# A two-layer encoder trunk: memory queries turned at tick 4, scores four ticks later, and ScalarE's weight splits queued behind data splits

## The chip, the cores and the metric

The kernel runs on one core of a Trainium2 chip. The metric is the device time of one execution in microseconds (us), the median of several runs. Five engines work side by side, each through its own instruction order: TensorE (PE; its weight loads are listed as PEld), VectorE (DVE), ScalarE (ACT), GpSimd (POOL) and SyncE (SP), which here issues the DMA transfers.

## The reference

The input is x, 256 tokens of width 2048, and 256 memory tokens. Two layers run one after the other, all in float32, and each sub-layer is wrapped in RMS norms before and after:

```python
for layer in range(2):
    hn = rms_norm(h, mix_pre_g[layer])
    if layer == 0:   # 8 neighbourhood heads and 8 sliding-window heads, one input projection
        y = concat(neighbourhood_attention(...), sliding_window_gqa(...)) @ even_w_out
    else:            # 8 heads of differential attention
        y = differential_attention(...) @ odd_w_out
    h = h + rms_norm(y, mix_post_g[layer])
    c = memory_cross_attention(rms_norm(h, mem_pre_g[layer]), rms_norm(mem, ...), wq, wk, wv, wo)
    h = h + rms_norm(c, mem_post_g[layer])
    f = squared_relu(rms_norm(h, mlp_pre_g[layer]) @ w_up) @ w_down      # d_ff = 8192
    h = h + rms_norm(f, mlp_post_g[layer])
```

The memory attention has four heads of 128: q from h, k and v from the memory tokens, a softmax over 256 memory tokens, and an output projection of 512 to 2048.

## The kernel before

**Arithmetic.** Every float32 operand of a matrix product is split in a high and a low part, and each product is three matmuls (`mm3`, L254: high times high, high times low, low times high). Data are split by `split_to` (L397): ScalarE writes the high part (L398), VectorE the low part (L399). Weights are split in `Weights.load` (L177): a DMA brings a tile of 256 x 512 into one of three raw buffers, ScalarE writes the high part and VectorE the low part into one of nine weight buffers `w` (L188 and L189 without a gain; L193 and L194, in two halves, with the gain of the norm multiplied in). A raw buffer is free again when both have read it.

**Blocks.** The tokens are two tiles of 128 (t = 0 and 1). `in_block` multiplies the transposed, normalized stream by one 512-column block of an input projection: eight weight tiles, for each token tile two steps of three matmuls per weight tile. With a lag, tile 1 runs that many weight tiles behind tile 0. `out_block` multiplies attention output or MLP output by 512 rows of an output projection: eight weight tiles, four chunks of 512 columns for each token tile; with `stagger` all chunks of tile 0 come first, and the chunk's result goes to `Leave`, which forms the norm and the new stream.

**Order.** TensorE's order is the order of the program, fixed by hand. A clock of ticks, one tick for a step of three matmuls, decides where small work comes between: `line.later(n, f)` runs f at n ticks from now, `line.when(n, ready, f)` tries at tick n and again each tick until ready, and `line.until(...)` runs what is due at once, with no matmuls between. The order on ScalarE, VectorE and SyncE is not written by hand: a planner takes, when the program is built, what it reckons to be ready, the earlier in the program first. It fixes one order per engine, and the engine then waits at each instruction for what that needs. So a weight split can be placed ahead of data splits that stand before it in the program.

**Weights ahead.** When TensorE's program uses weight tile j, `Weights.get` loads, in program order, up to tile j + 4 (`AHEAD`); at most nine are held.

**The memory block** (`mem_and_mlp`, L654, once per layer). First the query block, `in_block(U["mq", l], ...)` with a lag of 6. As a token tile is finished, `evac_T` (L417) has ScalarE write it, scaled, from PSUM to `q` (L427), and puts its turning `D_EVM` + t = 11 + t ticks later: four transposes on TensorE (L435) and a `split_to` into qT. Then `Heads(...).start(M_AT)`: the scores of head i at tick 8 + 5 i, if qT and kT are there (L257, at<-kT,qT), the softmax, and 9 ticks later the turning of the probabilities (`p_T`, L505) and its split into pT. The value block `mv` with a lag of 5 runs meanwhile, for 32 ticks; then for each head, once its pT has been issued, the mix of probabilities and values (L257, at<-pT,v) and its split into `lt`, then `out_block` of `mo`, staggered, and the MLP. The MLP has 16 groups: `up` makes 512 columns, `split_u` squares and splits them, and `out_block` of `dn` adds the group's output.

Of the kernel before, what the change touches and what calls it, by code (L numbers as in the profile page):

```python
# [3 lines left out]

# [1 line left out]

# [5 lines left out]
F32 = mybir.dt.float32  # L12
F32R = mybir.dt.float32r
BF16 = mybir.dt.bfloat16
AF = mybir.ActivationFunctionType
ALU = mybir.AluOpType
# [5 lines left out]
KT = D // P  # L22
# [12 lines left out]
SW_GAP, SW_T, SW_M = 4, 8, 7  # L35
NA_GAP, NA_T, NA_M = 5, 14, 9
ME_GAP, ME_T, ME_M = 5, 9, 12
D_TRS, D_RMS, D_EVM, D_EVU, M_TR, M_GO = 4, 13, 11, 6, 11, 1
A_ROPE, A_NA, M_AT = 10, 1, 8
A_DF, DF_GAP, DF_T, DF_M, DF_O = 6, 5, 7, 4, 8  # L40
AHEAD = 4
L_MQ, L_MV, L_UP, L_Q = 6, 5, 8, 6
# [29 lines left out]
def trunk(  # L72
# [6 lines left out]
    V, A, G, PE = nc.vector, nc.scalar, nc.gpsimd, nc.tensor  # L79
# [18 lines left out]
    gains = keep.tile([P, P], F32, name="gains")  # L98
# [4 lines left out]
    def mm_ps():  # L103
        return ps.tile([P, 512], F32, tag="mm", bufs=3, name="mm")

    def tr_ps():
        return ps.tile([P, 512], F32, tag="tr", bufs=2, name="tr")
# [15 lines left out]
    class Line:  # L123
        def __init__(self):
            self.now, self.q, self.n = 0, [], 0
# [29 lines left out]
    class Weights:  # L155
        def __init__(self):
            self.specs, self.tiles, self.n, self.wait, self.open = [], {}, 0, [], set()
            self.goal, self.live = -1, 0

        def plan_in(self, src, n0, g, spare=(), gate=None):  # L160

# [15 lines left out]
        def load(self, j):  # L177
            src, k0, n0, tag, _, g = self.specs[j]
            raw = rawp.tile([P, 2, 512], F32, tag="raw", name="raw")
            nc.sync.dma_start(  # L180
                raw, src[k0 * P : (k0 + 2) * P, n0 : n0 + 512].rearrange("(k p) n -> p k n", p=P)
            )
            if tag is None:
                w = wp.tile([P, 2, 2, 512], F32R, tag="w", name="w")
            else:
                w = sb.tile([P, 2, 2, 512], F32R, tag=tag, bufs=1, name="w")
            if g is None:
                A.copy(w[:, 0], raw)  # L188
                V.tensor_tensor(w[:, 1], raw, w[:, 0].bitcast(F32), ALU.subtract)  # L189
            else:  # L190
                for kk in range(2):
                    gk = gains[:, g * KT + k0 + kk : g * KT + k0 + kk + 1]
                    A.activation(w[:, 0, kk], raw[:, kk], AF.Copy, scale=gk)  # L193
                    V.scalar_tensor_tensor(  # L194
                        w[:, 1, kk], raw[:, kk], gk, w[:, 0, kk].bitcast(F32), ALU.mult, ALU.subtract
                    )
            self.tiles[j] = w

        def pump(self):
# [35 lines left out]
    W = Weights()  # L235
# [26 lines left out]
    def in_step(pt, u, kp, t):  # L262
        w = W.get(u + kp)
        line.until(lambda: I.has_x(t, kp // 2, W.specs[u + kp][5] >= G_MN))
        for kk in range(2):
            kt = 2 * kp + kk
            mm3(pt, xT_lhs(kt, t), lambda b: w[:, b, kk, :], kt == 0, kt == KT - 1)
            if kk == 1 and t == NT - 1:
                W.done(u + kp)
            line.tick()  # L270

    def in_block(u, evac, lag=0, between=None):

        pts = {}
        for i in range(8 + lag):
            for t, kp in enumerate((i, i - lag)):
                if not 0 <= kp < 8:
                    continue
                if kp == 0:
                    pts[t] = mm_ps()  # L280
                in_step(pts[t], u, kp, t)
                if kp == 7 and lag:
                    evac(t, pts[t])
                    if between is not None:
                        between(t)
        if not lag:
            for t in range(NT):
                evac(t, pts[t])
# [106 lines left out]


    def split_to(hi, lo, src):  # L397
        A.copy(hi, src)  # L398
        V.tensor_tensor(lo, src, hi.bitcast(F32), ALU.subtract)  # L399

    def scaled_split(dst, t, w, src, r):
# [5 lines left out]
    def rope(tile_, t, nh):  # L407
        v = tile_.rearrange("p (h d) -> p h d", d=DH)
        cos = cst[:, C_COS + t * 32 : C_COS + t * 32 + 32].unsqueeze(1).broadcast_to([P, nh, 32])
        sin = cst[:, C_SIN + t * 32 : C_SIN + t * 32 + 32].unsqueeze(1).broadcast_to([P, nh, 32])  # L410
        u = sb.tile([P, 4, 32], F32, tag="rope", bufs=1, name="rope")
        V.tensor_tensor(u[:, :nh, 0:16], v[:, :nh, 16:32], sin[:, :, 0:16], ALU.mult)
        V.tensor_tensor(u[:, :nh, 16:32], v[:, :nh, 0:16], sin[:, :, 16:32], ALU.mult)
        V.tensor_tensor(v[:, :nh, 0:32], v[:, :nh, 0:32], cos, ALU.mult)
        V.tensor_tensor(v[:, :nh, 0:32], v[:, :nh, 0:32], u[:, :nh], ALU.add)

    def evac_T(dst, r, q=False, roped=0, width=512, ev=None):  # L417


        def f(t, pt):  # L420
            rt = r[t]
            assert rt is not None
            if q:
                rt = sm.tile([P, 1], F32, tag="rs", name="rs", bufs=4)
                V.tensor_scalar_mul(rt, r[t], SCALE)
            u = sb.tile([P, 512], F32, tag="q", bufs=2, name="q")
            A.activation(u[:, :width], pt[:, :width], AF.Copy, scale=rt)  # L427
            if roped:
                rope(u[:, :width], t, roped)

            def turn():
                tp = tr_ps()
                n = width // P
                for i in range(n):
                    PE.transpose(tp[:, i * P : (i + 1) * P], u[:, i * P : (i + 1) * P], ident)  # L435
                d = [dst[:, a, t, 0:n, :].rearrange("p k c -> p (k c)") for a in range(2)]
                split_to(d[0], d[1], tp[:, :width])
                I.wrote(dst, t)

            line.later(D_ROPE + t if roped else (D_EV if ev is None else ev) + t, turn)  # L440

        return f
# [9 lines left out]
    def qT_tile():  # L452
        return sb.tile([P, 2, NT, 4, P], F32R, tag="qT", bufs=1, name="qT")

    def kT_tile():
        return sb.tile([P, 2, NT, 4, P], F32R, tag="kT", bufs=1, name="kT")

    def v_tile():
        return sb.tile([P, 2, NT, 512], F32R, tag="v", bufs=1, name="v")
# [39 lines left out]
    def p_T(p, tag="pT"):  # L499

        pT = sb.tile([P, 2, NT, S], F32R, tag=tag, bufs=2 if tag == "pT" else 1, name="pT")
        tp = at_ps()
        for t in range(NT):
            for kt in range(NT):
                PE.transpose(tp[:, kt * S + t * P : kt * S + (t + 1) * P], p[:, t, kt * P : (kt + 1) * P], ident)  # L505
        d = [pT[:, a].rearrange("p k q -> p (k q)") for a in range(2)]
        split_to(d[0], d[1], tp)
        return pT

    class Heads:  # L510
# [20 lines left out]
        def mix(self, i):  # L531
            v, vh = self.a[3], self.a[4]
            if self.lt is None:
                self.lt = lt_tile()
            o = at_ps()
            for kt in range(NT):
                mm3(
                    o[:, :S], lambda a: v[:, a, kt, vh(i) * DH : (vh(i) + 1) * DH],
                    lambda b: self.pT[i][:, b, kt, :], kt == 0, kt == NT - 1,
                )  # L540
            split_to(self.lt[:, 0, i, :], self.lt[:, 1, i, :], o[:, :S])
            self.n += 1
# [19 lines left out]
    U = {"kv": W.plan_in(w_in, 4096, G_MIX)}  # L562
# [91 lines left out]
    def mem_and_mlp(l, R, kT, nxt):  # L654
        qT = qT_tile()
# [2 lines left out]
            for n in range(4):  # L658
                mem_x(t, n)

        in_block(U["mq", l], evac_T(qT, R, q=True, ev=D_EVM), lag=L_MQ, between=between)
        v = v_tile()
        hd = Heads(qT, kT, lambda i: i, v, lambda i: i, tags=("pT", "pT", "qT", "kT"), lag=(ME_GAP, ME_T, ME_M)).start(M_AT, mix=False)
        in_block(U["mv", l], evac_V(v, RSM), lag=L_MV)
# [7 lines left out]
        R = lv.next  # L672
# [62 lines left out]
        for g in range(NG):  # L735
# [5 lines left out]
            if last:  # L741
                eps = []
                for r in R:
                    q = sm.tile([P, 1], F32, tag="r2", name="r2")
# [9 lines left out]
    R = [None] * NT  # L754
# [52 lines left out]
    qT = qT_tile()  # L807
# [13 lines left out]
    qT = qT_tile()  # L821
# [3 lines left out]
    qT = qT_tile()  # L825
# [9 lines left out]
    qT = qT_tile()  # L835
# [9 lines left out]
    W.free(("mq", 0))  # L845
    out_block(U["oa1"], hd.lt, False, lv, stagger=True)
    R = mem_and_mlp(0, lv.next, kT, G_MIX + 1)


# [85 lines left out]
    qT, kT, v = qT_tile(), kT_tile(), v_tile()  # L935
# [3 lines left out]
    for b in range(4):  # L939
        in_block(U["v", b], evac_V(v, R))  # L940
        hd = DiffHeads(qT, kT, v).start(A_DF)
        if b < 3:
            qT = qT_tile()
# [5 lines left out]
        else:  # L949
# [3 lines left out]
            W.free(("mq", 1))  # L953
            out_block(U["o3"], hd.lt, False, lv, stagger=True)
    mem_and_mlp(1, lv.next, kT, None)


# [27 lines left out]
```

## Time and profile before

| | |
|---|---|
| time, median of 3 runs | 2374.73 us (2373.03 to 2378.61) |
| the profiled execution's own time | 2374.78 us |
| its span (first to last instruction) | 2372.7 us |
| TensorE busy | 2346.2 us (99%), 11687 matmuls |
| VectorE busy | 1611.9 us (68%) |
| ScalarE busy | 1377.7 us (58%) |
| DMA | 451.88 MB, mean 190 GB/s |
| chain that ended last | PE 91%, DMA 3%, DVE 3%, ACT 2% |

A busy share is an average over stages. TensorE's matmuls are pipelined, so the distance from one start to the next tells how fast they are issued, and the duration shown is longer than that. In a timeline, the first two numbers are the start in us from the span's start and the length of the merged piece, and in brackets stands the idle time before it with what ended it.

### The profile page before, as it was taken

How to read it: one execution, taken by the hardware profiler on the slowest of the kernel's cores; microseconds unless marked ns; L12 is line 12 of the kernel's file. 1: busy time of each engine (PE TensorE's matmuls, PEld its weight loads, DVE VectorE, ACT ScalarE, POOL GpSimd, SP SyncE). 2: the span in 40 equal slices, each digit the busy share in tenths (PEclk: the TensorE clock that was granted, in tenths of full speed). 3: DMA queues.
4: the chain of work that ended last, by engine and by line, in shares of the span. 5: the costliest groups of instructions: out<-in, count | busy, mean ns of one | idle time of the engine just before them, and what ended most of it. 6: DMA issues, size and time to landing. Idle time of an engine off the chain costs nothing.

```text
span 2372.7 us, 32033 instructions
## 1 busy us (share of the span) xinstructions
PE 2346.2 (99%) x11687; PEld 1984.9 (84%) x11687; DVE 1611.9 (68%) x2545; ACT 1377.7 (58%) x2280; POOL 28.0 (1%) x46
## 2 busy tenths in 40 slices
PE   8999999999999999999999999999999999999998
PEld 7788887888888888888888888887888888888887
DVE  6776678856666656666876667788666666666666
ACT  6756567765545545545665655577655545555553
POOL 0000000000000000000000000000000000000000
PEclk9999999999999999999999999999999999999999
DMA  7657655565655666665565555655666665665663
GB/s 250 212 183 233 188 193 190 178 209 181 198 193 183 195 196 183 195 197 187 180 195 172 171 188 169 204 178 181 202 195 194 187 195 187 188 199 182 196 195 114
DMA packets 238279, 451.88 MB, mean 190 GB/s; under 512 B 21289, under 2 KB 22185, under 8 KB 237353
## 3 DMA queue, kind: packets, MB, share of 16 engines
q1 hardware_dynamic: 237832, 449.32, 59.7%
q8 instruction: 91, 1.49, 0.3%
q14 instruction: 68, 0.55, 0.1%
q10 hardware_dynamic: 288, 0.52, 0.1%
HBM read 445.59 MB, written 5.15 MB: 190 GB/s over the span
## 4 chain that ended last, share of the span: by engine, by line
PE 91%; DMA 3%; DVE 3%; ACT 2%; issue 1%; POOL 0%; SPq 0%; DVEq 0%; POOLq 0%; ACTq 0%
PE mm L257 59%; PE at L721 14%; PE at L725 7%; PE mm L721 5%; PE mm L725 2%; PE at L257 2%; DVE w L194 1%; DMA raw<-in_even_w_in 1%; PE tr L435 1%; DMA raw<-in_odd_w_in 1%; PE tr L348 1%; ACT w L193 1%; PE at L505 0%; DMA h<-in_x 0%; ACT junk L321 0%
## 5 line engine op out<-in xcount | busy, mean ns | idle before, releaser
L257 PE MATMUL mm<-w,lt 128*128 128x512 f32 x4032 | 926.9, 390 | 0.0
L257 PEld LDWEIGHTS mm<-w,lt 128*128 128x128 f32 x4032 | 754.8, 188 | 155.9
L194 DVE SCALAR_TENSOR_TENSOR w<-raw,gains,w 128x512 fp32r<-128x512 f32 x944 | 678.2, 747 | 261.5 <-ACT w L193 258.7
L193 ACT ACTIVATE w<-raw,gains 128x512 fp32r<-128x512 f32 x944 | 636.0, 717 | 354.1 <-PE mm L257 268.9
L257 PE MATMUL mm<-w,xT 128*128 128x512 f32 x2784 | 674.0, 395 | 2.0 <-DVE v L403 1.1
L189 DVE TENSOR_TENSOR w<-raw,w 128x1024 fp32r<-128x1024 f32 x336 | 411.2, 1224 | 377.6 <-ACT w L188 376.8
L188 ACT CAST w<-raw 128x1024 fp32r<-128x1024 f32 x336 | 353.1, 1051 | 439.1 <-PE mm L725 193.3
L257 PEld LDWEIGHTS mm<-w,xT 128*128 128x128 f32 x2784 | 513.2, 189 | 104.4 <-DVE v L403 1.9
L721 PE MATMUL at<-xT,w 128*128 128x512 f32 x1440 | 368.8, 391 | 0.0
L721 PEld LDWEIGHTS at<-xT,w 128*128 128x128 f32 x1440 | 262.7, 188 | 49.0
L725 PE MATMUL at<-xT,w 128*128 128x256 f32 x1440 | 211.0, 283 | 0.0
L725 PEld LDWEIGHTS at<-xT,w 128*128 128x128 f32 x1440 | 197.2, 191 | 9.4
L312 DVE TENSOR_TENSOR y<-mm,y 128x512 f32<-128x512 f32 x256 | 175.5, 685 | 15.6 <-PE mm L257 15.4
L721 PE MATMUL mm<-xT,w 128*128 128x512 f32 x480 | 147.8, 389 | 0.0
L721 PEld LDWEIGHTS mm<-xT,w 128*128 128x128 f32 x480 | 90.1, 188 | 19.3
L725 PE MATMUL mm<-xT,w 128*128 128x256 f32 x480 | 96.7, 283 | 0.0
L725 PEld LDWEIGHTS mm<-xT,w 128*128 128x128 f32 x480 | 74.9, 192 | 0.0
L679 ACT COPY ue<-at 128x256 f32<-128x256 f32 x90 | 33.7, 374 | 28.0 <-DVE s L680 13.9
L399 DVE TENSOR_TENSOR lt<-s,lt 128x512 fp32r<-128x512 f32 x64 | 44.1, 689 | 3.6 <-ACT lt L398 3.6
L257 PEld LDWEIGHTS at<-kT,qT 128*128 128x128 f32 x240 | 34.5, 191 | 10.5 <-ACT qT L398 4.2
L257 PE MATMUL at<-kT,qT 128*128 128x256 f32 x240 | 37.3, 288 | 5.8 <-ACT qT L398 3.4
L321 ACT ACTIVATE junk<-y 128x512 bf16<-128x512 f32 x32 | 20.1, 629 | 38.5 <-DVE y L307 38.3
(113 smaller groups left out, 1063.6 us busy)
## 6 DMA issues: line engine op xcount, KB each, us to landing
raw<-in_mlp_w_up SPq DMA_DIRECT2D x256, 512.0 KB, 4.1
raw<-in_mlp_w_down SPq DMA_DIRECT2D x256, 512.0 KB, 4.2
raw<-in_odd_w_in SPq DMA_DIRECT2D x96, 512.0 KB, 4.2
raw<-in_even_w_in SPq DMA_DIRECT2D x72, 512.0 KB, 4.3
raw<-in_even_w_out SPq DMA_DIRECT2D x32, 512.0 KB, 4.2
raw<-in_odd_w_out SPq DMA_DIRECT2D x32, 512.0 KB, 3.8
mt<-memT SPq DMA_DIRECT2D x32, 256.0 KB, 4.0
raw<-in_mem_wk SPq DMA_DIRECT2D x16, 512.0 KB, 4.4
```

Source lines behind the costliest of these rows:

```text
L188: A.copy(w[:, 0], raw)
L189: V.tensor_tensor(w[:, 1], raw, w[:, 0].bitcast(F32), ALU.subtract)
L193: A.activation(w[:, 0, kk], raw[:, kk], AF.Copy, scale=gk)
L194: V.scalar_tensor_tensor(w[:, 1, kk], raw[:, kk], gk, w[:, 0, kk].bitcast(F32), ALU.mult, ALU.subtract)
L257: PE.matmul(pt, lhs(a), rhs(b), start=first and i == 0, stop=last and i == 2)
L312: V.tensor_tensor(ysl, pt, ysl, ALU.add)
L348: PE.transpose(pt[:, i * P : (i + 1) * P], h[:, t, k * P : (k + 1) * P], ident)
L399: V.tensor_tensor(lo, src, hi.bitcast(F32), ALU.subtract)
L435: PE.transpose(tp[:, i * P : (i + 1) * P], u[:, i * P : (i + 1) * P], ident)
L679: A.copy(e, pt[:, S:])
L721: PE.matmul(pts[nt], wn, both, start=kp + kk == 0, stop=kp == 7 and kk == 1)
L725: PE.matmul(pts[nt][:, :S], wn, both[:, :S], start=False, stop=False)
```

## The change

Three things are changed. The memory queries' turning has its own delay, `D_EVQ` = 4 ticks (+ t) in place of 11. The memory heads' scores start at tick `M_AT` = 9 in place of 8. And `split_to` remembers its ScalarE instruction in `W.behind`; the splits of a weight tile loaded later in the program are put behind it with `tc.issue_after`. That gives each of the tile's ScalarE instructions an edge in issue order: the planner must place it after that instruction in ScalarE's order. It is no wait of its own, and VectorE's and SyncE's instructions get no edge. Every `split_to` counts: the turnings of q and k, the probabilities, the mixes and the MLP's `split_u`; `split_x` and `scaled_split` don't use it.

```diff
-D_TRS, D_RMS, D_EVM, D_EVU, M_TR, M_GO = 4, 13, 11, 6, 11, 1
-A_ROPE, A_NA, M_AT = 10, 1, 8
+D_TRS, D_RMS, D_EVM, D_EVQ, D_EVU, M_TR, M_GO = 4, 13, 11, 4, 6, 11, 1
+A_ROPE, A_NA, M_AT = 10, 1, 9
...
-            self.goal, self.live = -1, 0
+            self.goal, self.live, self.behind = -1, 0, None
...
-            if g is None:
-                A.copy(w[:, 0], raw)
-                V.tensor_tensor(w[:, 1], raw, w[:, 0].bitcast(F32), ALU.subtract)
-            else:
-                for kk in range(2):
...
+            with tc.issue_after(self.behind) if self.behind is not None else nullcontext():
+                if g is None:
+                    A.copy(w[:, 0], raw)
+                    V.tensor_tensor(w[:, 1], raw, w[:, 0].bitcast(F32), ALU.subtract)
+                else:
+                    for kk in range(2):
...
     def split_to(hi, lo, src):
-        A.copy(hi, src)
+        W.behind = A.copy(hi, src).ins
         V.tensor_tensor(lo, src, hi.bitcast(F32), ALU.subtract)
...
-        in_block(U["mq", l], evac_T(qT, R, q=True, ev=D_EVM), lag=L_MQ, between=between)
+        in_block(U["mq", l], evac_T(qT, R, q=True, ev=D_EVQ), lag=L_MQ, between=between)
```

## Rows read from the trace of the kernel before

**Rows 1.** The page: busy us, share of the span, instructions of each engine.
```profile
PE 2346.2 (99%) x11687; PEld 1984.9 (84%) x11687; DVE 1611.9 (68%) x2545; ACT 1377.7 (58%) x2280; POOL 28.0 (1%) x46
```

**Rows 2.** Waits of TensorE: who waits for whom: us in total, times, longest.
```profile
PE at L257 <- ACT qT L398: 3.4, 3, 1.7
```

**Rows 3.** Timeline of TensorE, layer 0, scores of the memory heads.
```profile
400.02 0.60 PE L257 MATMUL at<-kT,qT 128*128 128x256 f32 x3
...
403.96 0.85 PE L257 MATMUL mm<-w,xT 128*128 128x512 f32 x3
...
410.39 0.88 PE L257 MATMUL at<-kT,qT 128*128 128x256 f32 x6
411.10 2.23 PE L257 MATMUL mm<-w,xT 128*128 128x512 f32 x9
```

**Rows 4.** Timeline of TensorE, layer 1, the same place.
```profile
1607.96 0.60 PE L257 MATMUL at<-kT,qT 128*128 128x256 f32 x3
...
1611.53 0.86 PE L257 MATMUL mm<-w,xT 128*128 128x512 f32 x3
...
1616.37 0.88 PE L257 MATMUL at<-kT,qT 128*128 128x256 f32 x6
```

**Rows 5.** Stretches: us, TensorE busy, granted clock, DMA share, GB/s.
```profile
406.00:408.00 2.00, 2.00 (x6) 0.50 0.00 0
```

**Rows 6.** Timeline of ScalarE, layer 0, ahead of the second split of qT.
```profile
400.18 1.05 ACT L188 CAST w<-raw 128x1024 fp32r<-128x1024 f32 x1 [1.95 <-DMA raw<-in_mem_wo]
...
401.65 0.58 ACT L398 CAST qT<-tr 128x512 fp32r<-128x512 f32 x1
```

**Rows 7.** Timeline of layer 0, up to the first turning of memory queries.
```profile
382.72 6.42 PE L257 MATMUL mm<-w,xT 128*128 128x512 f32 x27
...
384.82 0.67 ACT L427 ACTIVATE q<-mm,rs 128x512 f32<-128x512 f32 x1
```

**Rows 8.** Timeline of ScalarE, layer 0, the second token tile's queries.
```profile
394.02 0.67 ACT L427 ACTIVATE q<-mm,rs 128x512 f32<-128x512 f32 x1
```

**Rows 9.** Timeline of layer 0, from head 3's turning to the output block.
```profile
422.79 0.60 PE L505 MATMUL at<-cst,p 128*128 128x128 f32 x4
...
424.38 0.68 DVE L399 TENSOR_TENSOR pT<-at,pT 128x512 fp32r<-128x512 f32 x1
...
424.51 1.82 PE L257 MATMUL at<-pT,v 128*128 128x256 f32 x13 [0.29 <-DVE v L403]
...
427.57 4.72 PE L257 MATMUL mm<-w,lt 128*128 128x512 f32 x20
...
428.31 0.35 ACT L398 CAST lt<-at 128x256 fp32r<-128x256 f32 x1
```

**Rows 10.** Timeline of VectorE; then the page's DMA issues: count, KB, us to landing.
```profile
425.13 1.23 DVE L189 TENSOR_TENSOR w<-raw,w 128x1024 fp32r<-128x1024 f32 x1
...
raw<-in_mlp_w_down SPq DMA_DIRECT2D x256, 512.0 KB, 4.2
```

**Rows 11.** Stretches (PE, PEld, DVE, ACT, POOL busy); L189 and L398 by line.
```profile
343.00:357.00 14.00, 14.00 (x68) 11.55 (x67) 10.21 (x19) 6.83 (x16) 0.48 (x1) 1.00 0.22 76
357.00:371.00 14.00, 14.00 (x71) 11.59 (x70) 13.56 (x24) 11.47 (x25) 0.99 (x2) 1.00 0.26 82
...
1549.50:1565.00 15.50, 15.50 (x74) 12.79 (x73) 10.61 (x18) 7.76 (x17) 0.48 (x1) 1.00 0.46 147
...
L189 DVE TENSOR_TENSOR w<-raw,w x5: 1221/1226/1226, 324.8 to 338.6; 128x1024 fp32r<-128x1024 f32 x5
...
L398 ACT CAST lt<-at x2: 360/372/383, 342.6 to 342.8; 128x256 fp32r<-128x256 f32 x2
```

**Rows 12.** Timeline of one MLP group: a down block on TensorE, split_u's last CAST.
```profile
718.30 21.92 PE L257 MATMUL mm<-w,lt 128*128 128x512 f32 x96
...
723.57 0.60 ACT L398 CAST lt<-s 128x512 fp32r<-128x512 f32 x1
```

**Rows 13.** Timeline of TensorE in the first attention stage, two of its waits.
```profile
68.86 0.98 PE L257 MATMUL at<-kT,qT 128*128 128x256 f32 x4 [0.47 <-DVE qT L399]
...
92.03 0.86 PE L257 MATMUL at<-pT,v 128*128 128x256 f32 x5 [0.85 <-DVE pT L399]
```

More of the change, by code (lines that the diff above doesn't have):

```diff
@@ L2 @@
 import math
-from contextlib import ExitStack
+from contextlib import ExitStack, nullcontext
 import numpy as np
@@ L186, in load @@
                 w = sb.tile([P, 2, 2, 512], F32R, tag=tag, bufs=1, name="w")
-            if g is None:
-                A.copy(w[:, 0], raw)
-                V.tensor_tensor(w[:, 1], raw, w[:, 0].bitcast(F32), ALU.subtract)
-            else:
-                for kk in range(2):
[L192 to L196, printed above, removed]
+            with tc.issue_after(self.behind) if self.behind is not None else nullcontext():
[4 more added lines that the diff above has]
+                    for kk in range(2):
+                        gk = gains[:, g * KT + k0 + kk : g * KT + k0 + kk + 1]
+                        A.activation(w[:, 0, kk], raw[:, kk], AF.Copy, scale=gk)
+                        V.scalar_tensor_tensor(
+                            w[:, 1, kk], raw[:, kk], gk, w[:, 0, kk].bitcast(F32), ALU.mult, ALU.subtract
+                        )
             self.tiles[j] = w
```

## The prediction

> **What bounds the kernel.** Read first the busy row of the page: TensorE is busy 2346.2 of a span of 2372.7 us [rows 1], so all edits together can win at most the 26.5 us in which it is not, and start and tail hold most of these. Only a changed hole on TensorE counts. Next come TensorE's own waits: the longest past the start is the one for ScalarE's split of qT [rows 2]. They lie where the change acts, in the memory block of each layer. In TensorE's timeline of layer 0 the six score matmuls of head 0 start right behind the turning of the queries (400.02), and the next tick's work starts only at 403.96 [rows 3]; in layer 1 it is 1607.96 to 1611.53 [rows 4]. Last, read the clock: after layer 0's hole the granted clock is 0.50, the lower level [rows 5]; after layer 1's it stays full. A fixed order rules TensorE, so a hole there is paid in full.
>
> A tick is 0.68 us: 96 matmuls of 512 columns are issued in 21.92 us [rows 12], 0.227 us each, three to a tick. Six of 256 columns take 0.71 us (410.39 to 411.10, [rows 3]), 0.12 us each.
>
> **The scores' wait goes.** Before, tile 1 is turned 12 ticks after the query block's end, and head 0's scores, due at tick 8, retry until that same tick. After, it is turned at tick 5 and scored at tick 9: four ticks, 2.7 us, lie between. What must fit in there is the split of one tile, 0.58 us on ScalarE and 0.68 us on VectorE (durations of [rows 6] and [rows 9]); in before that split also stood behind a weight split of 1.05 us [rows 6], which the new order puts behind it. So I take the wait as gone (bounds: all of it, or 1 us left per layer). Layer 0: 3.94 us for work of 0.71, saved 3.2. Layer 1: 3.57, saved 2.9. Then the clock: from 403.96 to 410.39 are 6.43 us [rows 3], the same 24 matmuls in layer 1, 1611.53 to 1616.37, 4.84 us [rows 4]: 1.6 saved. Sum -7.7.
>
> The Trainium skill, "TensorE: Matmul & The Clock Gate", Part 1, says that the full clock is released by activity and taken back when the array idles. The rows agree in part: layer 0's hole was followed by half clock, layer 1's, only 0.37 us shorter, was not. By that rule the new holes below could cost clock too, 1.6 us each by layer 0's rows; each is half of layer 1's hole or less, which left the clock alone, so the sum carries no clock term for them.
>
> **Turning too early.** The transposes at tick 4 read q, ScalarE's scaled copy out of PSUM. Tile 0: the 27 matmuls from 382.72 are nine ticks up to the turn at tick 11, so tick 4 falls two ticks behind 382.72, at 384.08; q is written from 384.82 to 385.49 [rows 7]. TensorE would stand 1.4 us. Nothing in the change brings q forward: its place in ScalarE's order is behind weight splits that the new edge doesn't touch, and VectorE, which prepares its factor, is full there. Layer 1 repeats the pattern, so 2 x 1.4 = +2.8 (bounds 0, if the planner moves q up; 4, if what is late below delays q as well). Tile 1: the block ends 12 ticks and a turn ahead of 400.02, at 391.5; tick 5 is 394.9, and q is done at 394.02 + 0.67 = 394.69 [rows 8]: 0.
>
> **Head 3 falls off the value block.** That block has 32 ticks. Before, the heads' scores run at 12, 13, 18, 23 and their turns nine ticks later, the last at 32, inside the block. After: 9, 14, 19, 24, turns 18, 23, 28, 33. Head 3's turn now comes between mix 2 and mix 3, and mix 3 waits for its split with nothing to cover it. From [rows 9]: mix 0's last matmul waits for v and runs at 424.51 in either case; mixes 1 and 2 end at 424.63 + 12 x 0.12 = 426.07; transposes 0.60 to 426.67; the split, 0.58 [rows 6] and 0.68, with hand-overs to 428.0; five matmuls 0.60: the output block starts at 428.6 instead of 427.57, +1.0. Twice: +2.0 (bounds 0 and 4).
>
> **Weights queued behind.** The edge is put on each weight tile that is loaded, in program order, behind a split of attention or MLP data; loads come four tiles ahead of their use in that order, while the trace runs them further ahead, so many splits move later. Where the tile is used at the usual rate this is hidden by the lead that is left. Example, the MLP: tile 4 of a down block must now follow the CAST of 723.57 (+0.60); ScalarE 1.05 and VectorE 1.23 bring it to 726.5 [rows 6, 10]; it is used after 48 matmuls, at 718.30 + 10.9 = 729.2 [rows 12]. A lead of 2.7 us remains: 0, for all 30 such groups (bounds 0 and 0.5 each; above that only if the planner also misplaces it).
>
> Two places are tighter. (a) The memory output block, token half first, uses a tile every six matmuls, 1.36 us. Tiles 4 to 6 lie raw in all three raw buffers until head 3's last split, 1.1 us after the block starts (428.31 + 0.35 against 427.57, [rows 9]); tile 4's split ends at 1.1 + 1.05 + 1.23 = 3.4, tile 7's transfer takes its buffer, 4.2 us [rows 10], to 7.6, its split to 9.9; it is used at 7 x 1.36 = 9.5. +0.4, twice: +0.8 (bounds 0 and 3). (b) The block oa1 in front of the memory queries: VectorE does the weight splits of its last four tiles (1.23 us each) up to 338.6 + 1.23 = 339.8, and the lt splits that they must now follow come at 342.6 to 342.8 [rows 11]. So 4.9 us more work falls in 343 to 357, where VectorE idles 3.8 of 14; the next 14 us leave it 0.4 [rows 11]. The surplus of 1.1 us is carried to the query tiles, which TensorE uses as they come: +1.1. In layer 1 the stretch is longer and VectorE idles 4.9 of 15.5 [rows 11], as much as is added: 0 there (bounds of both together: 0 and 8).
>
> Where the edge helps: in the first attention stage TensorE waited 0.47 us for VectorE's half of qT and 0.85 us for that of pT [rows 13]; weight work placed behind such splits leaves the engines to them. -1.3 (bounds 0 and -1.3).
>
> **Sum.** -7.7 + 2.8 + 2.0 + 0.8 + 1.1 - 1.3 = -2.3 us on the profiled execution's own 2374.78 us: 2372.5. That execution is 0.05 us above the median of the runs, so nothing is added. No data moves more and no matmul is added.
>
> **Rivals.**
> 1. The planner writes q early enough, and the displaced splits find gaps: without the +2.8, +0.8 and +1.1 the sum is -7.0: 2367.8. For it: the first turn's stall rests on an order that is written anew. Against: VectorE has 0.4 us free around it [rows 11].
> 2. Slower: VectorE becomes the bound between the mixer's output block and the memory queries. Place: 343 to 380 and its twin; price: all 4 x 1.23 us in both layers and none of it in gaps, 9.8 in place of 1.1, +6.4: 2381.2. It decides once the added splits stand behind the residual updates instead of in the gaps in front of them. For it: the 13.56 of 14 busy. Against: 3.8 us free just ahead.
> 3. Slower: the MLP loses its lead. If the edge pushes tile 4 past its use by 0.5 us in each of 30 groups, +15: 2387.5. Against: the 2.7 us of lead worked out above, and ScalarE gets its three interleaved weight splits out of the way first.
> 4. The change doesn't do what it says: another instruction still stands in front of qT's split, and the scores wait as before. Then -2.3 + 7.7 = +5.4: 2380.2. Against: four ticks are twice what the split takes.
>
> **Chances.** The forecast with its neighbours 0.60, rival 1 0.18, rival 2 0.10, rival 3 0.05, rival 4 0.07. About 0.2%, 4.7 us, is what a measurement can tell from no change. Half of rival 4's outcomes and the mildest of rival 2 stay within it. So faster 0.20, same 0.62, slower 0.18. The range runs from rival 1's 2367.8, a little under, to 2379.5, short of rivals 2 to 4; the forecast's own range is 2369.5 to 2376.
>
> **What would show it.** Right: TensorE's waits for qT at the scores gone in both layers, and the clock full at 400 to 410. A new hole of about 1.4 us in front of the first turning of memory queries, waiting for q, and one of about 1 us in front of head 3's mix, waiting for pT. Weight splits behind the lt, qT and pT splits on ScalarE, with the MLP's period per group unchanged. Wrong: a longer MLP period; holes over 2 us at the memory query tiles with VectorE as releaser; no hole at the turning.

## The result and the profile after

The changed kernel takes 2414.14 us, the median of 4 runs (2413.53 to 2416.51); the kernel before, run beside it, takes 2374.56 (2373.03 to 2378.61). The ratio is 1.0163 (95% interval 1.0149 to 1.0178): 39.6 us slower, where 2372.5 was forecast. The span of the profiled execution is 2412.5 us, against 2372.7.

The page after: the busy row [rows 1], and from its groups (busy us, mean ns of one | idle time in front of them, and what ended most of it) the two forms of weight split on ScalarE.

```profile
PE 2357.2 (98%) x11687; PEld 1988.2 (82%) x11687; DVE 1612.6 (67%) x2545; ACT 1378.8 (57%) x2280; POOL 29.4 (1%) x46
...
L194 ACT ACTIVATE w<-raw,gains 128x512 fp32r<-128x512 f32 x944 | 631.7, 719 | 333.4 <-DMA raw<-in_mlp_w_up 188.1
L189 ACT CAST w<-raw 128x1024 fp32r<-128x1024 f32 x336 | 346.8, 1052 | 282.9 <-DMA raw<-in_mlp_w_down 233.4
```

The same two groups of the page before, one line number lower:

```profile
L193 ACT ACTIVATE w<-raw,gains 128x512 fp32r<-128x512 f32 x944 | 636.0, 717 | 354.1 <-PE mm L257 268.9
L188 ACT CAST w<-raw 128x1024 fp32r<-128x1024 f32 x336 | 353.1, 1051 | 439.1 <-PE mm L725 193.3
```

No engine has more work: the counts are equal and the busy times nearly so, except that TensorE's grew by 11 us. What changed is whom ScalarE waits for at a weight split. Before, it was TensorE: all nine weight buffers were full, and a split waited until one came free. After, it is the transfer into the raw buffer. Loading has gone from "as far ahead as the buffers allow" to "just as the data arrive". Over all such lines, ScalarE's waits for raw transfers add up to 95.6 us before and 560.6 us after (some 395 of these in the two MLPs). SyncE's transfers in turn wait for a raw buffer to come free; the waits of its queue after (us in total, times, longest), with VectorE's half of a weight split as releaser, without a gain and with one:

```profile
SPq L180 <- DVE w L190: 859.1, 314, 20.2
SPq L180 <- DVE w L195: 857.7, 431, 16.6
```

The same waits before, one line number lower:

```profile
SPq L180 <- DVE w L194: 1061.9, 442, 14.6
SPq L180 <- DVE w L189: 558.8, 264, 4.5
```

For splits without a gain the longest grew from 4.5 to 20.2 us, but the two lines together hardly differ, 1620.7 us before and 1716.8 after: in both kernels the queue mostly waits for the next raw buffer, so these sums don't show lateness. The start of a transfer, measured against TensorE's first use of its tile, does. For the 24 tiles of the first three output blocks of the differential attention it lay 28.7 us ahead of the use before and 19.5 after (medians), for the MLP's down blocks 27.6 and 19.7.

TensorE's waits after:

```profile
PE mm L258 <- DVE v L404: 14.4, 6, 5.5
PE tr L349 <- DVE h L389: 11.0, 5, 5.4
...
PE tr L436 <- ACT q L428: 2.1, 2, 1.5
```

The first two are where the time is, and neither is a wait for a weight. v is the value block's (and the mixer's) result on its way out of PSUM, h the new stream after a norm. Before, TensorE waited for these two 1.7 us in all; after, 26.9 (all lines that name v or h counted, here and below). To place the loss, the start of the same matmul was compared in both traces; in us lost per stretch (times of the kernel before, past the first 100 us, where executions differ anyway):

| stretch | after | the two tick numbers alone (e1) | the edge alone (e2) |
|---|---|---|---|
| 200–345, mixer of layer 0 | +4.3 | −0.6 | +4.4 |
| 345–380, oa1 to memory queries | +2.0 | 0.0 | +2.1 |
| 380–392, first turning | +0.7 | +1.3 | 0.0 |
| 392–412, scores | −4.8 | −4.7 | +1.4 |
| 412–430, head 3 and mixes | +1.4 | +3.7 | −0.7 |
| 430–470, memory output block | +1.6 | 0.0 | +2.7 |
| 470–1115, MLP | 0.0 | 0.0 | 0.0 |
| 1115–1200, end of the MLP, start of layer 1 | +7.9 | −0.1 | +7.5 |
| 1200–1550, differential attention | +20.4 | +0.4 | +21.0 |
| 1550–1590, before layer 1's memory queries | +1.5 | 0.0 | +1.7 |
| 1590–1600, first turning | +1.7 | +2.0 | 0.0 |
| 1600–1620, scores | −2.7 | −2.3 | +4.0 |
| 1620–1635, head 3 and mixes | +1.3 | +2.7 | −0.7 |
| 1635–1660, memory output block | +1.9 | 0.0 | +2.0 |

The memory block with the blocks just ahead of it, which the forecast was about, comes out at +4.6 over both layers. 32.6 us lie in three stretches that the forecast gave no term. (The traced execution of e2 took 2422.19 us, 4 less than its median; its column is that much short.)

Three of the holes, in timelines of all engines after (start, length, and in brackets the idle time before and its releaser): the end of layer 0's MLP, a block of the differential attention, and its last one.

```profile
1158.08 2.77 ACT L194 ACTIVATE w<-raw,gains 128x512 fp32r<-128x512 f32 x4 [1.11 <-DMA raw<-in_odd_w_in]
1158.84 0.75 DVE L195 SCALAR_TENSOR_TENSOR w<-raw,gains,w 128x512 fp32r<-128x512 f32 x1 [0.98 <-ACT w L194]
...
1160.29 1.28 DVE L308 TENSOR_TENSOR y<-mm,y 128x512 f32<-128x512 f32 x2
...
1163.40 2.74 DVE L389 SCALAR_TENSOR_TENSOR h<-y,rr,h 128x512 f32<-128x512 f32 x4 [0.44 <-POOL rr L326]
...
1164.21 1.12 PE L349 MATMUL tr<-cst,h 128*128 128x128 f32 x4 [5.41 <-DVE h L389]
...
1239.63 1.34 ACT L194 ACTIVATE w<-raw,gains 128x512 fp32r<-128x512 f32 x2 [1.28 <-DMA raw<-in_odd_w_in]
...
1242.52 1.34 ACT L194 ACTIVATE w<-raw,gains 128x512 fp32r<-128x512 f32 x2 [1.54 <-DMA raw<-in_odd_w_in]
...
1244.28 0.72 ACT L194 ACTIVATE w<-raw,gains 128x512 fp32r<-128x512 f32 x1 [0.42 <-DMA raw<-in_odd_w_in]
1244.91 0.67 ACT L403 ACTIVATE v<-mm,rr 128x512 fp32r<-128x512 f32 x1
...
1245.70 0.74 DVE L404 SCALAR_TENSOR_TENSOR v<-mm,rr,v 128x512 fp32r<-128x512 f32 x1
...
1246.50 3.91 PE L258 MATMUL mm<-w,xT 128*128 128x512 f32 x9 [2.18 <-DVE v L404]
...
1546.41 2.56 ACT L194 ACTIVATE w<-raw,gains 128x512 fp32r<-128x512 f32 x4
1550.04 0.62 ACT L341 CAST xT<-mt 128x512 fp32r<-128x512 f32 x1 [1.07 <-DMA mt<-memT]
1550.57 0.68 ACT L403 ACTIVATE v<-mm,rr 128x512 fp32r<-128x512 f32 x1
1551.30 0.75 DVE L404 SCALAR_TENSOR_TENSOR v<-mm,rr,v 128x512 fp32r<-128x512 f32 x1
...
1552.10 1.22 PE L258 MATMUL mm<-w,xT 128*128 128x512 f32 x2 [5.50 <-DVE v L404]
```

Read the middle one: ScalarE stands idle three times for raw data (1.28, 1.54, 0.42 us), each time at a weight split that TensorE needs only much later. The copy of v out of PSUM stands behind these in ScalarE's order; it starts at 1244.91, VectorE's half follows, and TensorE has stood 2.18 us. At 1550 ScalarE waits 1.07 us for a copy of memory tokens whose transfer came late, in the same queue; an earlier such copy, at 1545.89, had waited 2.44 us.

The longer holes also cost clock. Stretches of TensorE after (us, TensorE busy, granted clock, DMA share, GB/s):

```profile
1164.00:1168.00 4.00, 3.79 (x11) 0.50 0.01 2
...
1552.00:1556.00 4.00, 3.90 (x9) 0.50 0.39 139
```

Behind the two holes of 5.4 and 5.5 us the clock is 0.50, its lower level (1.2 GHz). It fell behind two of 2.3 us too, at 216.5 and 1243.9. In all, 31 matmuls of 512 columns ran at the lower level, against 6 before, which is 6.2 against 1.2 us lost: 5.0 of the loss. With the 25.2 us of added waits for v and h that is some 30 of the 39.6; the rest, in shorter waits and at the start and the tail, was not followed up.

### The profile page after: what moved, and what is told of

It reads as the page before. It is cut to its first block, busy times and chain, and to the rows that moved or that the text cites. A ratio compares the mean times of both kernels' runs of the same rounds, so it can differ in the third digit from the quotient of the medians.

```text
span 2412.5 us, 31863 instructions
## 1 busy us (share of the span) xinstructions
PE 2357.2 (98%) x11687; PEld 1988.2 (82%) x11687; DVE 1612.6 (67%) x2545; ACT 1378.8 (57%) x2280; POOL 29.4 (1%) x46
## 3 DMA queue, kind: packets, MB, share of 16 engines
q8 instruction: 92, 1.51, 0.2%
## 4 chain that ended last, share of the span: by engine, by line
PE 77%; DMA 9%; DVE 8%; ACT 4%; issue 1%; POOL 0%; ACTq 0%; DVEq 0%; POOLq 0%; SPq 0%
PE mm L258 45%; PE at L722 14%; PE at L726 7%; PE mm L722 4%; DVE w L195 3%; DMA raw<-in_odd_w_in 3%; PE mm L726 2%; PE at L258 2%; ACT w L194 2%; DMA raw<-in_even_w_in 2%; DVE w L190 1%; DMA raw<-in_mlp_w_down 1%; DMA raw<-in_mlp_w_up 1%; DVE h L389 1%; DMA raw<-in_mem_wk 1%
## 5 line engine op out<-in xcount | busy, mean ns | idle before, releaser
L195 DVE SCALAR_TENSOR_TENSOR w<-raw,gains,w 128x512 fp32r<-128x512 f32 x944 | 665.8, 748 | 202.7 <-ACT w L194 201.2
L258 PE MATMUL mm<-w,xT 128*128 128x512 f32 x2784 | 681.2, 397 | 15.4 <-DVE v L404 14.4
L189 ACT CAST w<-raw 128x1024 fp32r<-128x1024 f32 x336 | 346.8, 1052 | 282.9 <-DMA raw<-in_mlp_w_down 233.4
L681 DVE TENSOR_TENSOR s<-at,ue 128x256 f32<-128x256 f32 x90 | 38.2, 425 | 121.4 <-ACT ue L680 119.3
L488 ACT ACTIVATE p<-at,nm 128x256 f32<-128x256 f32 x48 | 22.4, 471 | 48.8 <-DVE nm L485 48.8
L326 POOL TENSOR_TENSOR rr<-rb,mhalf 128x1 f32<-128x1 f32 x26 | 20.4, 786 | 1997.3 <-DVE rb L384 1710.7
```

Source lines behind the costliest of these rows:

```text
L195: V.scalar_tensor_tensor(w[:, 1, kk], raw[:, kk], gk, w[:, 0, kk].bitcast(F32), ALU.mult, ALU.subtract)
L258: PE.matmul(pt, lhs(a), rhs(b), start=first and i == 0, stop=last and i == 2)
L681: V.tensor_tensor(s[:, i * S : (i + 1) * S], pt[:, :S], e, ALU.add)
```

## The experiments

In the table, "before" is the kernel before on the same chip; ratios have 95% intervals. A control is the same edit with the two tick numbers but without the edge.

| run | median us | before | ratio |
|---|---|---|---|
| e1_ticks | 2376.59 | 2375.9 | 1.0004 (0.9994 to 1.0014) |
| e2_edge | 2426.2 | 2375.9 | 1.0219 (1.0202 to 1.0237) |
| e4_local | 2379.27 | 2375.9 | 1.0017 (1.0007 to 1.0027) |
| e8_nomlp | 2405.18 | 2374.91 | 1.0126 (1.0112 to 1.0139) |
| e7_raw5 | 2386.34 | 2374.91 | 1.0043 (1.0029 to 1.0057) |
| e10_free_raw5, control | 2387.2 | 2375.69 | 1.0045 (1.0029 to 1.0061) |
| e3_ahead8 | 2402.7 | 2375.9 | 1.0119 (1.0104 to 1.0135) |
| e5_free_ahead8, control | 2404.78 | 2374.91 | 1.0121 (1.0107 to 1.0135) |
| e11_ahead6 | 2403.0 | 2374.47 | 1.0121 (1.0106 to 1.0136) |
| e12_free_ahead6, control | 2400.09 | 2374.47 | 1.0108 (1.0091 to 1.0125) |
| e6_ticks6 | 2382.04 | 2374.91 | 1.0029 (1.0019 to 1.0039) |
| e9_best | 2377.73 | 2375.69 | 1.0007 (0.9998 to 1.0016) |

**Which part costs.** e1_ticks is the kernel before with the two tick numbers only; e2_edge is the changed kernel with the old two.

```diff
 e1_ticks, against before
+D_EVQ = 4, and in_block(U["mq", l], ..., ev=D_EVQ)
-M_AT = 8
+M_AT = 9
 e2_edge, against after
-D_EVQ, M_AT = 4, 9
+D_EVQ, M_AT = 11, 8
```

> The kernel before with the tick changes alone (queries turned at tick 4, scores from tick 9), no edge. Theory A (the edge halves the lead of the weight splits, and data copies that stand behind late weight splits on ScalarE and VectorE hold TensorE up): the ticks by themselves cost nothing, 2369 to 2375 us. Rival B (the ticks shift the planner's whole order): 2390 or more. Either way a hole of about 1 us in front of the first turning of memory queries and about 1 us at head 3's mix.

> The changed kernel with both tick numbers set back (turned at 11, scores from 8), the edge kept. Theory A: 2412 to 2422 us, all of the loss and the scores' wait on top. Rival B: 2370 to 2378.

The tick numbers alone change nothing that can be measured; the edge alone costs 2.2%, more than the whole change and a little above the expected range. The stretch table shows that the two hardly meet outside the memory block: there the edge alone has scores that cost 1.4 and 4.0 us, which the later scores of the full change take away.

**Which splits' edge costs.** e4_local lets `split_to` set `W.behind` only from the memory query block to the end of the value block. e8_nomlp leaves out the MLP's `split_u` and keeps all other marks.

```diff
 e4_local, against after
-        W.behind = A.copy(hi, src).ins
+        i = A.copy(hi, src).ins
+        if W.mark:      # True ahead of in_block(mq); False, and behind = None, after in_block(mv)
+            W.behind = i
 e8_nomlp, against after
-    def split_to(hi, lo, src):
-        W.behind = A.copy(hi, src).ins
+    def split_to(hi, lo, src, mark=True):      # the MLP's splits pass False
+        i = A.copy(hi, src).ins
+        if mark:
+            W.behind = i
```

> The changed kernel with the edge kept only for tiles that are loaded during the memory block's query and value blocks (splits of qT and pT there); everywhere else weights are free. Theory A: the scores' wait gone without the late copies, 2366 to 2373 us. Rival C: a loss in the memory output block and the MLP's start remains, 2376 or more.

> The changed kernel, but the MLP's splits are not marked: weights are put behind turned and mixed attention data alone. Theory A: the 8.4 us lost where the first MLP ends go, those in the attention stages stay: 2402 to 2409 us. If the MLP's edges are of no matter: 2412 to 2418.

With the marks kept to the place of the change, 35 of the 39.6 us are gone. At 2379.27 us e4 still lies above the expected 2366 to 2373, but not by the rival's mechanism: the memory output blocks lose 0.0 and 0.4 us and the MLP's start nothing. What pays back the scores' gain is the first turning (1.1 and 1.8) and head 3 with the mixes (2.1 and 5.0). Without the MLP's marks, 9.0 are gone (2414.14 to 2405.18): the end of the MLP loses 0.5 instead of 7.9 us, while the differential attention still loses 20.8. So the MLP's marks slow its own end and not the attention behind it. (The mixer of layer 0 loses 1.3 instead of 4.3, though it lies ahead of the MLP. About half of the difference is clock: the changed kernel has a stretch at the lower level there, at 219 us, and e8 has none. The rest was not followed up.) The waits of TensorE in e8 keep v in first place:

```profile
PE mm L258 <- DVE v L406: 11.8, 6, 4.1
PE tr L349 <- DVE h L389: 7.2, 5, 2.2
```

**How it costs.** My theory after the result: the splits that wait for their mark hold the three raw buffers; transfers start late; ScalarE and VectorE then stand at late weight splits, with data copies behind them. More raw buffers, or loads further ahead in the program, should then take the loss away. The rival was that the order itself, splits placed behind data, makes the data late. (The planner fixes the orders of ScalarE, VectorE and SyncE anew in every run, so none of these runs changes the transfers alone.) e7_raw5 gives the changed kernel five raw buffers (and eight weight buffers, for room); e10_free_raw5 is its control.

```diff
 e7_raw5, against after; e10_free_raw5, the same against e1_ticks
-NW = 9
+NW = 8
-    rawp = ctx.enter_context(tc.tile_pool(name="rawp", bufs=3))
+    rawp = ctx.enter_context(tc.tile_pool(name="rawp", bufs=5))
```

> The changed kernel with five raw buffers in place of three and eight weight buffers in place of nine (the same memory). If the loss comes by way of raw buffers that wait for a split behind the edge, so that the next transfers start late (theory A): at most 2395 us, and ScalarE's waits for transfers under half of the changed kernel's. If raw buffers are no link (rival D: the copies are late by their mere place on ScalarE): 2408 to 2420.

> The control to the run with five raw buffers: five raw and eight weight buffers, ticks 4 and 9, no edge. Theory A: the 8 us that the memory queries lost there belong to the ninth weight buffer's absence, not to the edge, and the edge with five raw buffers costs 2 to 6 us: this control 2380 to 2385 us. If five raw buffers merely speed everything up: 2368 to 2375, and the edge still costs 11 or more.

With five raw buffers the edge costs 2386.34 − 2387.2 = −0.9 us, where with three it costs 2414.14 − 2376.59 = 37.6; the control came out above the 2380 to 2385 that I had expected. ScalarE's waits for raw transfers fall from 560.6 to 82.9 us, and TensorE's for v and h from 26.9 to 7.2 (control: 5.4). Three waits of e7, of ScalarE and of TensorE:

```profile
ACT w L194 <- DMA raw<-in_mlp_w_up: 55.8, 76, 1.3
```

```profile
PE tr L349 <- DVE h L389: 4.6, 2, 2.5
...
PE mm L258 <- DVE v L404: 1.1, 3, 0.5
```

The same with loads further ahead: `AHEAD` of 8 and of 6 in place of 4, each with its control.

```diff
 e3_ahead8 and e11_ahead6, against after; e5_free_ahead8 and e12_free_ahead6, the same against e1_ticks
-AHEAD = 4
+AHEAD = 8      # e11, e12: 6
```

> The changed kernel with weights loaded eight tiles ahead in program order in place of four, so that a tile's edge goes to an earlier split. Theory A: the lead comes back, 2370 to 2390 us, and ScalarE's waits for the raw transfers shrink to under half. Rival C (to stand behind data splits costs in itself, whatever the lead): 2408 to 2418.

> The control to the run with the edge and loads eight tiles ahead: ticks 4 and 9, loads eight ahead, no edge. That run lost 27 us, but elsewhere than the changed kernel (start and memory queries). Theory A: this control loses the same, 2396 to 2406 us, so that with a lead of eight tiles the edge itself costs under 5. Rival C (part of the edge's cost is left at a lead of eight): 2376 to 2390.

> The changed kernel with loads six tiles ahead, between the four of the change (edge costs 38 us against the ticks alone) and the eight (nothing against its control). Theory A: in between, the edge costs 10 to 25 us against the control sent with it, and its waits for v and h lie between those of the two. If there is a step and not a slope: under 5 or over 33.

> The control: ticks 4 and 9, loads six ahead, no edge. Between the 2376 of four ahead and the 2405 of eight ahead, 2378 to 2395 us; were the edge's cost a matter of the load order alone, this control would lose as much as the run with the edge.

By itself e3, 1.2% slower and above the 2370 to 2390 us that I had expected, looks as if a longer lead helped only in part. Its control is as slow: loading eight ahead costs 1.2% without any edge, and the edge adds 2402.7 − 2404.78 = −2.1 us. At six it adds 2403.0 − 2400.09 = +2.9. I had expected some 10 to 25 us at six, and a control near 2378 to 2395; both missed.

In these totals the price looks like a step, but they hide a gain: at head 3 and the mixes the edge gives back some 6 us with five raw buffers and some 9 at six ahead, against the controls. By stretches, matmul by matmul as in the table above, the price is a slope. The second column is the median start of a transfer ahead of its tile's first use, in the first three output blocks of the differential attention:

| edge against its control | start ahead of use, us: control, edge | edge's price in the differential attention, us | with mixer of layer 0 and end of the MLP |
|---|---|---|---|
| four ahead, three raw buffers (after, e1) | 28.7, 19.5 | 20.0 | 32.9 |
| six ahead (e11, e12) | 28.7, 24.0 | 5.7 | 11.4 |
| five raw buffers (e7, e10) | 32.0, 24.4 | 4.7 | 5.5 |
| eight ahead (e3, e5) | 28.7, 28.5 | 1.0 | 1.8 |

The later the transfers start, the more the attention loses. (One trace of each run; the four controls differ in this stretch by up to 1.0 us among themselves, so the last row is no more than that.) e8, whose marks differ only in the MLP, fits too: 19.5 us there, and the attention loses 20.8; in its down blocks, without marks, the start is back at 27.6, and the MLP's end loses 0.5.

At six ScalarE's waits for raw transfers are still 482.9 us in sum (control 108.4), but some 370 of them lie in the MLPs, which lose nothing. The sum of these waits isn't what decides, but whether a data copy stands behind one of them when it is needed.

**A better version?** e6_ticks6 has no edge, and turning and scores at later ticks, so that q is written in time; e9_best adds the edge, kept to the memory block.

```diff
 e6_ticks6, against before
-ME_GAP, M_AT = 5, 8
+ME_GAP, M_AT = 4, 11
+D_EVQ = 6
 e9_best: the same numbers in e4_local, with behind = None only after the memory output block
```

> No edge; queries turned at tick 6, memory scores from tick 11 and four ticks apart (11, 15, 19, 23), turns nine later (20, 24, 28, 32, the last inside the value block). If the ticks' gain was paid back by the first turning's wait for q (1.4 and 2.0 us) and by head 3's turn outside the block (3.7 and 2.7 us): 2365 to 2370 us. If what was paid back comes from the planner's new order in general: 2374 to 2380.

> Meant as a version that beats both: queries turned at tick 6, memory scores at 11, 15, 19, 23, and the edge only where it helped, from the splits of memory queries and probabilities to weight tiles loaded in the memory block. No wait for q at the turning, head 3's turn inside the value block, no weight split in front of qT, v and pT: 7 us off the scores, nothing paid back, 2366 to 2371 us. If the transfers of memory tokens in front of qT hold the scores up as in the run at tick 6 without the edge: 2373 to 2382.

e6 is 0.3% slower, above both ranges that I had put down. The wait for q is gone (the first turnings lose 0.0 and 0.3 us), but now the mechanism of rival 4 is there: at the scores ScalarE's split of qT stands behind a weight split and a copy of memory tokens. Timeline of e6, layer 0:

```profile
401.54 1.05 ACT L188 CAST w<-raw 128x1024 fp32r<-128x1024 f32 x1
402.87 0.62 ACT L340 CAST xT<-mt 128x512 fp32r<-128x512 f32 x1 [0.29 <-DMA mt<-memT]
403.40 0.58 ACT L398 CAST qT<-tr 128x512 fp32r<-128x512 f32 x1
...
404.03 0.51 PE L257 MATMUL at<-kT,qT 128*128 128x256 f32 x2 [1.35 <-ACT qT L398]
...
424.12 1.04 ACT L188 CAST w<-raw 128x1024 fp32r<-128x1024 f32 x1 [1.59 <-DMA raw<-in_mem_wo]
425.07 0.68 ACT L402 ACTIVATE v<-mm,rsm 128x512 fp32r<-128x512 f32 x1
...
425.80 0.50 PE L257 MATMUL at<-pT,v 128*128 128x256 f32 x2 [1.58 <-ACT v L402]
```

At 424.12 the pattern of the whole case stands in a kernel without an edge: ScalarE waits 1.59 us for a raw tile, the copy of v is next in its order, and TensorE loses 1.58. e9's edge takes the weight splits away from that place, not the copies of memory tokens, and it ends level with before. No version here beats the kernel before.

## Why the prediction was wrong

**The step that failed: "Weights queued behind".** It priced a later weight split only by the moment when TensorE uses that tile, and called the rest hidden "by the lead that is left". That part held: the lead, from the end of a weight split to its tile's first use, fell from 19.5 to 8.9 us (median of the tiles of the MLP's down blocks) and from 20.2 to 10.8 in the first three output blocks of the differential attention, and in no stretch past the start did TensorE wait for a weight tile. What had no term is what the lead paid for besides, and three stretches without a term lost 32.6 us. A split that waits for its turn holds one of three raw buffers, so its successors' transfers start late; ScalarE and VectorE take their instructions in order, so a split whose data are still on the way holds up the copies behind it, and these have no lead at all. Experiments e7, e10, e11, e12, e3 and e5 show the first link: with more raw buffers, or loads further ahead, transfers start earlier, and the price of the edge in the attention falls from 20.0 to 4.7, 5.7 and 1.0 us. The second is seen in the timelines at 1158, 1244 and 1550 and was not isolated; no run moved the data copies to another engine. The rows on which the step rested were those of a stretch with full weight buffers; "splits that wait keep raw buffers" stood in the prediction for the memory output block alone, as (a), and belonged to every stage with a mark.

**Rival 2 and rival 3** had the right sign and the wrong place. The two blocks ahead of the memory queries lost 2.0 and 1.5 us, where rival 2 put 9.8. The MLP's period didn't move: after, the down blocks of 21.92 us start at 723.28 and 767.31, 44.03 apart, and before at 718.3 and 762.3; in the timeline after, the example of the prediction reads

```profile
723.28 21.92 PE L258 MATMUL mm<-w,lt 128*128 128x512 f32 x96
...
726.53 0.62 ACT L399 CAST lt<-s 128x512 fp32r<-128x512 f32 x1
727.06 2.95 ACT L189 CAST w<-raw 128x1024 fp32r<-128x1024 f32 x3
...
733.23 1.05 ACT L189 CAST w<-raw 128x1024 fp32r<-128x1024 f32 x1 [3.22 <-DMA raw<-in_mlp_w_down]
...
767.31 21.92 PE L258 MATMUL mm<-w,lt 128*128 128x512 f32 x96
```

The splits stand behind the last CAST, as foreseen, and the fourth waits 3.22 us for its transfer [rows 12]. The MLP can afford it: TensorE works 21.9 us at a stretch and its copies have time. It is the MLP's end and the attention blocks, where each copy is waited for, that can't.

**The scores' wait**, −7.7 with the clock: −4.8 and −2.7, so −7.5. Right, and by the mechanism named. In layer 0 the scores now follow the ticks without a hole, and the clock is full from 395 to 420 us [rows 3, 5]:

```profile
390.95 0.66 PE L436 MATMUL tr<-cst,q 128*128 128x128 f32 x4 [0.55 <-ACT q L428]
...
401.69 0.60 PE L436 MATMUL tr<-cst,q 128*128 128x128 f32 x4
...
404.90 0.88 PE L258 MATMUL at<-kT,qT 128*128 128x256 f32 x6
405.61 3.59 PE L258 MATMUL mm<-w,xT 128*128 128x512 f32 x15
```

**The first turning**, +2.8: TensorE waited 0.55 and 1.51 us for q, and the stretches lost 0.7 and 1.7; without the edge 1.3 and 2.0. Right within its bounds, and the release was as named [rows 7].

**Head 3**, +2.0: 1.4 and 1.3 with the edge. In layer 0 mix 3 waits for both halves of pT, one behind the other [rows 9]:

```profile
428.27 0.60 PE L506 MATMUL at<-cst,p 128*128 128x128 f32 x4
429.54 0.38 PE L258 MATMUL at<-pT,v 128*128 128x256 f32 x1 [0.68 <-ACT pT L399]
430.27 0.86 PE L258 MATMUL at<-pT,v 128*128 128x256 f32 x5 [0.34 <-DVE pT L400]
430.97 4.27 PE L258 MATMUL mm<-w,lt 128*128 128x512 f32 x18
```

Without the edge the stretch costs 3.7 and 2.7, more than the term; that is why the tick numbers alone gain nothing: −7.0 at the scores, +3.3 at the turning, +6.4 at head 3.

**Memory output block**, +0.8, and **oa1** with its twin in layer 1, +1.1: 3.5 and 3.5 were lost. Too small by a factor of four and of three, and not by the mechanism described: in all four places TensorE waited for h, with holes of 1.35 and 1.87 us at the memory output block and 1.75 and 1.27 at the other, and not for a late weight tile. This is the failed step again.

**The clock.** The sum had no clock term for new holes, because each was to be at most half as long as the one that had left the clock alone. The holes that came were longer and lay elsewhere, and the lower level took 5.0 us.

The −1.3 of the first attention stage can't be told from what two executions of the same order differ in there.

## What to carry to other kernels

A prefetched operand's lead is not only its own: it keeps the in-order engines that prepare it from ever standing still, and with that the copies queued behind. So when a change delays such work, ask how much later its transfers will start, and what stands behind the next instruction that will wait for one; and before an ordering edge is put into a helper, list all stages that call it. To judge such an edge at another depth of buffers, run that depth without the edge too: e3 alone would have been misread by 29 us. And compare by stretches: here a gain in one place hid the price in another.

## What had not been expected of the hardware

Loading six or eight tiles ahead instead of four costs 24 and 28 us by itself (2400.09 and 2404.78 against 2376.59, without an edge); the traces show longer waits at the start, at the memory queries and at the head's end, and why was not settled.

A hole's length doesn't tell whether the clock falls. After, the hole of 2.34 us at 1243.9 was followed by a granted clock of 0.52, one of 2.38 us at a block of the same kind later in the same attention (1445.8) by 1.00:

```profile
1246.50:1250.00 3.50, 3.50 (x9) 0.52 0.77 247
...
1448.50:1452.00 3.50, 3.50 (x18) 1.00 0.61 192
```

Six holes of 1.3 to 1.9 us left it alone (366, 448, 1348, 1602, 1629 and 1687 us), the two of over 5 us did not, nor did one of 2.31 us at 216.5 (0.54 behind it). The Trainium skill, "TensorE: Matmul & The Clock Gate", Part 1, says that an idle array loses the full clock; these rows agree for the long holes and show both outcomes near 2.3 us.
